# Gate columns, first load buffers and the sums of w_down in a hybrid decoder block

## The chip, the cores and the metric

The kernel runs on one core of one Trainium2 chip. The metric is the device time of one execution in microseconds (us), the median of several runs. The engines of the core are TensorE (PE; its weight loads are listed as PEld), VectorE (DVE), ScalarE (ACT), GpSimd (POOL) and SyncE (SP, which here only issues transfers). Sixteen DMA engines move the data for the queues of SP and POOL.

## What is computed

One layer of a hybrid decoder on x of 512 rows and 1024 columns, float32. Cut to what matters:

```
h = rms_norm(x, norm_mix_g);  p = h @ w_in                  # 1024 x 8208
q_a, k_a, v_a, o_a, i_a, f_a, q_b, k_b, v_b, g_a, g_b = split(p)
y_a = sigmoid(o_a) * head_norm(mlstm(silu(conv(q_a, k_a)), v_a, i_a + b_i, f_a + b_f))
y_b = stick_breaking(head_norm(q_b), head_norm(k_b), v_b)
x = x + (sigmoid(g_a + b) * y_a + sigmoid(g_b + b) * y_b) @ w_out
x = x + square(relu(rms_norm(x, norm_mlp_g) @ w_up)) @ w_down   # 1024 -> 4096 -> 1024
```

## The kernel before

Every float32 matmul operand is cut into a high and a low part in the matmul format (`hi` by a cast on ACT, `lo` by a subtraction on DVE), and a product is made of three matmuls (`mm3`, lines 103 to 105): high by high, high by low, low by high. A slice of weights (256 rows by 512 columns, 512 KB) is loaded by SP into a `raw` buffer, of which there are two, and cut into `whi` and `wlo`, of which there are four each (`stage`, lines 88 to 100).

**The start.** Line 193 loads the gate columns of w_in (16 columns of 1024 rows, tile `wg_r`) on POOL's queue, behind some small vectors. Lines 206 to 210 load the four row tiles of x and, between them, the four slices of the value projection va0 on SP's queue; slices 2 and 3 wait for the buffers of 0 and 1. `norm_rows(t)` normalises row tile t, transposes it on TensorE and cuts it into `hT`. va0 is a product of four parts, one for each row tile, each over all four slices; lines 293 to 303 set norms, parts and gates in their order. `gates` multiplies `hT` by the gate weights `wg`, makes running sums and maxima on DVE and ACT, writes eight rows to DRAM (`rows`) and leaves; each head then has its row broadcast to 128 partitions by POOL's queue (`rb<-rows`, line 363) and takes exponentials of it (line 371). The projections qka0 and qka1 follow va0; each holds four PSUM banks (`pp`, four in all) until ACT has copied them out (`xc`, line 324).

**The MLP.** Four blocks g of 1024 hidden columns. `up(i)` makes 512 hidden columns (i = 0 to 7): 96 matmuls in two halves, then rectifies, squares and cuts the result, with sums and differences of its quadrants, into `ue` (holds A11 and A12), `uf` (A22), `ta` (S1, S4) and `tb` (S2, S3). `down(g)` multiplies by w_down in the Winograd form of Strassen's scheme: seven products instead of eight, each of 24 matmuls, with the numbers and operands of `PRODUCTS` (line 34). The four quadrants B11, B12, B21, B22 of w_down are loaded, each as two slices of 512 KB, into eight buffers `raw_B`; where a product needs a difference of two of them, DVE subtracts in place (line 713), 32 subtractions in all. `parts` (lines 685 to 690) cuts a slice into `whi_p` and `wlo_p`. The sums collect in PSUM in the pairs of banks x, z and y and are added by DVE to the result `acc` or to `s1` (line 730). `ORDER_DOWN` sets the order of the products; 0 stands for the next block's `up(2g+2)`, which is put into the middle of the block, and 9, in the last block, for the additions of s1 to three quadrants.

Within these rules a planner sets the order of the instructions on each engine ahead of time, by priorities (order in the program, less an offset) and by its own simulated times; each engine then runs its list in order.

Of the kernel before, what the change touches and what calls it, by code (L numbers as in the profile page):

```python
# [8 lines left out]
F32 = mybir.dt.float32  # L9
F32R = mybir.dt.float32r  # L10
AF = mybir.ActivationFunctionType
ALU = mybir.AluOpType
# [4 lines left out]
P = 128  # L17
S = 512
D = 1024
NT = S // P  # L20
NK = D // P
# [7 lines left out]
AHEAD = 1500  # L29
# [1 line left out]
NWARM = 5  # L31


PRODUCTS = {1: ("A11", "B11", None, "x", None), 2: ("A12", "B21", None, "x", (0, 0)),
# [3 lines left out]

ORDER_DOWN = (5, 1, 0, 2, 6, 3, 7, 4)
ORDER_LAST = (5, 1, 2, 6, 9, 3, 7, 4)  # L40
C_QA, C_KA, C_VA, C_OA, C_I, C_F = 0, 512, 1024, 2048, 3072, 3080
C_QB, C_KB, C_VB, C_GA, C_GB = 3088, 4112, 5136, 6160, 7184

# [6 lines left out]
def block_kernel(ctx: ExitStack, tc: tile.TileContext, x, norm_mix_g, w_in, b_if, b_gate, conv_w, mlstm_norm_g,  # L50
                 sb_q_norm_g, sb_k_norm_g, w_out, norm_mlp_g, w_up, w_down, out):
    nc = tc.nc
    act, dve, pool, pe = nc.scalar, nc.vector, nc.gpsimd, nc.tensor
# [31 lines left out]

    last = {}

    def stage(k2, srcs, name, ahead=None):

        with tc.high_priority(offset=AHEAD if ahead is None else ahead):  # L90
            raw = wp.tile([P, 2, 512], F32, tag="raw", name=f"raw_{name}{k2}", bufs=2)
            for c, ap in srcs:
                n = ap.shape[-1]
                last["load"] = nc.sync.dma_start(out=raw[:, :, c:c + n],
                                                 in_=ap.rearrange("(kk p) n -> p kk n", p=P)).ins
            hi = wp.tile([P, 2, 512], F32R, tag="whi", name=f"whi_{name}{k2}")
            lo = wp.tile([P, 2, 512], F32R, tag="wlo", name=f"wlo_{name}{k2}")
            act.copy(hi, raw)  # L98
            dve.tensor_sub(lo, raw, hi.bitcast(F32))  # L99
        return hi, lo  # L100
# [88 lines left out]
    nc.gpsimd.dma_start(out=bif[0:8, :], in_=b_if[0, 0:8].rearrange("(p o) -> p o", o=1))  # L189
    nc.gpsimd.dma_start(out=bif[32:40, :], in_=b_if[0, 8:16].rearrange("(p o) -> p o", o=1))  # L190
    vec = cst.tile([P, NV], F32, name="vec")
    wr = cv.tile([P, NK, 16], F32, name="wg_r")
    nc.gpsimd.dma_start(out=wr, in_=w_in[0, :, C_I:C_I + 16].rearrange("(k p) n -> p k n", p=P))

    def col(i):
        return vec[:, i:i + 1]
# [9 lines left out]
    for t in range(NT):  # L206
        xt = xp.tile([P, D], F32, name=f"x_{t}")
        nc.sync.dma_start(out=xt, in_=x[0, t * P:(t + 1) * P, :])
        xs.append(xt)
        va0_w.append(stage(t, va0_src(t), "va0", 0))  # L210
    def norm_rows(t):
        jk = xp.tile([P, D], F32, tag="nx", name=f"jk{t}", bufs=3)
        r = sm.tile([P, 1], F32, tag="r1", name=f"r{t}")
# [78 lines left out]

    norm_rows(0)
    norm_rows(1)
    wg = gate_weights()
    va0 = chunk("va0", None, False, staged=va0_w, evac=v_evac(v0, "va0"), gen=True)
    next(va0)
    norm_rows(2)
    next(va0)
    norm_rows(3)  # L300
    next(va0)
    cc, rows, em = gates(wg)
    next(va0)
# [331 lines left out]
    def up(i):  # L635

        ws, got = [stage(k2, rows2(w_up, 0, i * S)(k2), f"up{i}") for k2 in range(4)], []
        for j in range(2):
            acc = {o: ps_proj.tile([P, S], F32, tag="pp", name=f"pp_up{i}{o}") for o in (j, j + 2)}
            for k in range(NK):  # L640
                for o in acc:
                    sl, (wh, wl) = slice(o * P, (o + 1) * P), ws[k // 2]
                    mm3(acc[o], wh[:, k % 2, sl], wl[:, k % 2, sl], hT[0][:, k, :], hT[1][:, k, :], k == 0, k == NK - 1)
            u = mp.tile([P, 2, S], F32, tag="ur", name=f"ur{i}{j}", bufs=2)
            for w in range(2):
                dve.scalar_tensor_tensor(u[:, w, :], acc[j + 2 * w], 0.0, rw, ALU.max, ALU.mult)  # L646
                act.activation(u[:, w, :], u[:, w, :], AF.Square)  # L647
            e = r4.tile([P, 2, S], F32R, tag="r4", name=f"ue{i}{j}")
            for w in range(2):
                act.copy(e[:, 0, w * 256:w * 256 + 256], u[:, w, HA])  # L650
            e3 = e[:, :, :].rearrange("p x (w n) -> p x w n", w=2)
            dve.tensor_sub(e3[:, 1], u[:, :, HA], e3[:, 0].bitcast(F32))
            f = mp.tile([P, 2, 256], F32R, tag="a22", name=f"uf{i}{j}", bufs=6)
            split(f, u[:, 1, HB])
            sa = big.tile([P, S], F32, tag=f"ya{3 + j}", name=f"sa{i}{j}")
            sb = big.tile([P, S], F32, tag=f"ya{5 + j}", name=f"sb{i}{j}")
            dve.tensor_add(sa[:, HA], u[:, 0, HB], u[:, 1, HB])
            dve.tensor_sub(sb[:, HA], sa[:, HA], u[:, 0, HA])
            dve.tensor_sub(sb[:, HB], u[:, 0, HA], u[:, 0, HB])
            dve.tensor_sub(sa[:, HB], u[:, 1, HA], sb[:, HA])  # L660
            ta = r4.tile([P, 2, S], F32R, tag="r4", name=f"ta{i}{j}")
            split(ta, sa)
            tb = r4.tile([P, 2, S], F32R, tag="r4", name=f"tb{i}{j}")
            made = split(tb, sb)
            got.append({"made": made, "A11": e[:, :, HA], "A12": e[:, :, HB], "A22": f[:, :, :], "S1": ta[:, :, HA],
                        "S4": ta[:, :, HB], "S2": tb[:, :, HA], "S3": tb[:, :, HB]})
        return got

    def quad(r, c, t):
        return acc_t[2 * r + t][:, c * S:(c + 1) * S]  # L670

    def down(g, u):
        raw = {}
        with ExitStack() as es:
            es.enter_context(tc.high_priority(offset=AHEAD))
            if g == 0:
                es.enter_context(tc.issue_after(wo_load))
            for n, r, c in (("B11", 0, 0), ("B12", 0, 1), ("B21", 1, 0), ("B22", 1, 1)):
                for j in range(2):
                    r0 = g * D + (4 * j + 2 * r) * P  # L680
                    raw[n, j] = mp.tile([P, 2, S], F32, tag="rawd", name=f"raw_{n}{g}{j}", bufs=8)
                    nc.sync.dma_start(out=raw[n, j], in_=w_down[0, r0:r0 + 256, c * S:(c + 1) * S]
                                      .rearrange("(kk p) n -> p kk n", p=P))

        def parts(n, t):
            hi = wp.tile([P, 2, S], F32R, tag="whi", name=f"whi_{n}")
            lo = wp.tile([P, 2, S], F32R, tag="wlo", name=f"wlo_{n}")
            act.copy(hi, t)  # L688
            dve.tensor_sub(lo, t, hi.bitcast(F32))  # L689
            return hi, lo  # L690

        order = ORDER_LAST if g == 3 else ORDER_DOWN
        adds = [PRODUCTS[n][4] for n in order if n in PRODUCTS]
        sums = {}
        for n in order:
            if n == 0:
                yield
                continue
            if n == 9:
                for r, c in ((0, 1), (1, 1), (1, 0)):  # L700
                    for t in range(2):
                        dve.tensor_add(quad(r, c, t), quad(r, c, t), s1[t])
                continue
            a, b, diff, to, q = PRODUCTS[n]
            adds.pop(0)
            if diff:
                with ExitStack() as es:
                    if g == 0:
                        es.enter_context(tc.issue_after(last["wo"]))
                    if (g, n) == (3, 4):  # L710
                        es.enter_context(tc.issue_after(u[-1]["made"]))
                    for j in range(2):
                        dve.tensor_sub(raw[b, j], raw[diff[0], j], raw[diff[1], j])  # L713
            with tc.high_priority(offset=AHEAD):
                w = [parts(f"p{n}{g}{j}", raw[b, j]) for j in range(2)]
            start = to not in sums
            if start:
                sums[to] = [bank(f"{to}{g}{t}") for t in range(2)]
            for t in range(2):
                sl = slice(t * P, (t + 1) * P)  # L720
                for p in range(4):
                    (hi, lo), A, kk = w[p // 2], u[p][a], p % 2
                    mm3(sums[to][t], A[:, 0, sl], A[:, 1, sl], hi[:, kk, :], lo[:, kk, :], start and p == 0, p == 3,
                        skip_group_check=True)
            for t in range(2):
                o = s1[t] if q is None else quad(*q, t)
                if n == 1 and g == 0:
                    act.copy(o, sums[to][t])
                else:
                    dve.tensor_add(o, o, sums[to][t])  # L730
                if g == 3 and q and q not in adds:
                    r0, c0 = (2 * q[0] + t) * P, q[1] * S
                    nc.sync.dma_start(out=out[0, r0:r0 + P, c0:c0 + S], in_=o)

    u = up(0) + up(1)
    for g in range(4):
# [31 lines left out]
```

## Time and profile before

| | us |
|---|---|
| median of 3 runs | 848.1 (847.83 to 849.15) |
| the profiled execution | 849.74 |
| its span, first to last instruction | 848.0 |
| TensorE busy | 827.2 |
| DVE busy | 598.6 |
| ACT busy | 408.3 |
| mean granted TensorE clock | 0.992 |

The profile is one execution as the hardware recorded it. Its times are from the start of the span. "Busy" adds up the durations of an engine's instructions. A row of the timeline has start, length, engine, line, operation, what is written from what is read, and in brackets how long the engine stood idle before it and what ended that. TensorE's matmuls overlap, so a matmul of 0.39 us does not mean that the next one starts 0.39 us later.

### The profile page before, as it was taken

The page shows a single profiled execution, that of the slowest core. Times are in us where ns is not written, and L with a number is a line of the kernel's source. Part 1 is how long each engine was busy: PE and PEld are TensorE (multiplying, and loading weights), DVE is VectorE, ACT ScalarE, POOL GpSimd, SP SyncE. Part 2 cuts the span into 40 slices and gives each one's busy share as a digit, 9 for nine tenths or more (in the row PEclk, how much of TensorE's full clock was granted, in tenths as well). Part 3 has the DMA queues.
Part 4 walks back from the last instruction along what each step waited for, and adds up shares of the span by engine and source line. Part 5 has one row for each costly group of instructions (what it writes and reads, how often), then busy time and mean ns, then how long its engine had stood idle before and what let it go on. Part 6 is the DMA issues. An engine that isn't in the chain of part 4 may idle for free.

```text
span 848.0 us, 10083 instructions
## 1 busy us (share of the span) xinstructions
PE 827.2 (98%) x3798; PEld 682.1 (80%) x3798; DVE 598.6 (71%) x808; ACT 408.3 (48%) x619; POOL 84.2 (10%) x150
## 2 busy tenths in 40 slices
PE   5997999999999999999999999999999999999998
PEld 3875888688888788888888888888888888888876
DVE  3484999688647688457465646786958795888695
ACT  4434756846435645355354345553524453453441
POOL 3003045222302011001001100000000000000000
PEclk9998999999999999999999999999999999999999
DMA  7235233333122233222131384211531252226001
GB/s 172 81 102 174 94 116 100 133 95 132 55 99 72 78 83 104 88 83 92 51 120 54 102 321 125 75 48 54 173 124 54 78 183 83 74 75 198 2 25 75
DMA packets 48530, 85.76 MB, mean 101 GB/s; under 512 B 3337, under 2 KB 15673, under 8 KB 48482
## 3 DMA queue, kind: packets, MB, share of 16 engines
q1 hardware_dynamic: 46434, 77.64, 28.8%
q0 software_dynamic: 2048, 7.48, 3.3%
q8 instruction: 30, 0.49, 0.2%
q14 instruction: 18, 0.15, 0.1%
HBM read 82.94 MB, written 2.17 MB: 100 GB/s over the span
## 4 chain that ended last, share of the span: by engine, by line
PE 90%; DMA 4%; DVE 2%; ACT 2%; issue 1%; POOL 1%; SPq 0%; POOLq 0%; ACTq 0%; DVEq 0%
PE pp_up L103 7%; PE pp_up L104 7%; PE pp_up L105 7%; PE pp_qkb L103 3%; PE pp_qkb L104 3%; PE pp_qkb L105 3%; PE y L103 3%; PE y L105 3%; PE y L104 3%; DMA raw_va<-in_w_in_dram 2%; DMA rb<-rows 2%; PE pp_ga L103 2%; PE pp_wo L103 2%; PE pp_ga L105 2%; PE pp_vb L103 2%; PE pp_vb L105 2%
## 5 line engine op out<-in xcount | busy, mean ns | idle before, releaser
L103 PE MATMUL pp_up<-hT,whi_up 128*128 128x512 f32 x256 | 99.3, 390 | 0.0
L104 PE MATMUL pp_up<-hT,whi_up 128*128 128x512 f32 x256 | 99.2, 389 | 0.0
L105 PE MATMUL pp_up<-hT,wlo_up 128*128 128x512 f32 x256 | 94.0, 389 | 0.0
L688 ACT CAST whi_p<-raw_B 128x1024 fp32r<-128x1024 f32 x56 | 59.0, 1055 | 58.4 <-PE pp_up L104 37.8
L689 DVE TENSOR_TENSOR wlo_p<-raw_B,whi_p 128x1024 fp32r<-128x1024 f32 x56 | 68.0, 1221 | 18.0 <-ACT whi_p L688 10.0
L98 ACT CAST whi_up<-raw_up 128x1024 fp32r<-128x1024 f32 x32 | 33.7, 1053 | 60.8 <-PE y L105 28.8
L103 PEld LDWEIGHTS pp_up<-hT,whi_up 128*128 128x128 f32 x256 | 48.0, 188 | 10.5 <-ACT whi_up L98 0.6
L105 PEld LDWEIGHTS pp_up<-hT,wlo_up 128*128 128x128 f32 x256 | 48.1, 188 | 10.0
L104 PEld LDWEIGHTS pp_up<-hT,whi_up 128*128 128x128 f32 x256 | 48.1, 188 | 9.8
L99 DVE TENSOR_TENSOR wlo_up<-raw_up,whi_up 128x1024 fp32r<-128x1024 f32 x32 | 39.1, 1222 | 18.9 <-ACT whi_up L98 18.7
L104 PE MATMUL pp_qkb<-wlo_qkb,hT 128*128 128x512 f32 x128 | 50.0, 391 | 0.0
L103 PE MATMUL pp_qkb<-whi_qkb,hT 128*128 128x512 f32 x128 | 49.8, 393 | 0.2 <-DVE va L161 0.2
L105 PE MATMUL pp_qkb<-whi_qkb,hT 128*128 128x512 f32 x128 | 49.5, 391 | 0.0
L478 POOL TENSOR_SCALAR_AFFINE_SELECT b<-b 128x128 f32<-128x128 f32 x32 | 21.2, 679 | 192.7 <-ACT b L475 115.6
L713 DVE TENSOR_TENSOR raw_B<-raw_B,raw_B 128x1024 f32<-128x1024 f32 x32 | 38.8, 1219 | 0.2
L647 ACT ACTIVATE ur<-ur 128x512 f32<-128x512 f32 x32 | 19.5, 629 | 33.3 <-DVE ur L646 32.9
L483 DVE TENSOR_TENSOR_SCAN r<-r,msk 128x512 f32<-128x512 f32 (+3 forms) x32 | 25.5, 835 | 10.1 <-ACT r L474 10.1
L103 PE MATMUL pp_qka<-hT,whi_qka 128*128 128x512 f32 x64 | 26.0, 408 | 6.2 <-ACT xc L324 6.2
L103 PE MATMUL pp_va<-whi_va,hT 128*128 128x512 f32 x64 | 25.8, 411 | 4.7 <-ACT whi_va L98 4.7
L646 DVE SCALAR_TENSOR_TENSOR ur<-pp_up,rw 128x512 f32<-128x512 f32 x32 | 21.1, 687 | 11.4 <-PE pp_up L105 11.4
L105 PEld LDWEIGHTS pp_qkb<-whi_qkb,hT 128*128 128x128 f32 x128 | 24.0, 188 | 5.6
L103 PEld LDWEIGHTS pp_qkb<-whi_qkb,hT 128*128 128x128 f32 x128 | 24.0, 188 | 5.5 <-DVE va L161 0.5
(286 smaller groups left out, 2235.7 us busy)
## 6 DMA issues: line engine op xcount, KB each, us to landing
raw_B<-in_w_down_dram SPq DMA_DIRECT2D x32, 512.0 KB, 4.2
raw_up<-in_w_up_dram SPq DMA_DIRECT2D x32, 512.0 KB, 4.1
raw_qkb<-in_w_in_dram SPq DMA_DIRECT2D x32, 256.0 KB, 3.8
rb<-rows POOLq DMA_DIRECT2D x8, 640.0 KB, 5.1
raw_va<-in_w_in_dram SPq DMA_DIRECT2D x8, 512.0 KB, 6.7
raw_qka<-in_w_in_dram SPq DMA_DIRECT2D x16, 256.0 KB, 4.7
raw_vb<-in_w_in_dram SPq DMA_DIRECT2D x8, 512.0 KB, 4.1
raw_oa<-in_w_in_dram SPq DMA_DIRECT2D x8, 512.0 KB, 4.0
```

What stands on the lines that cost most here:

```text
L98: act.copy(hi, raw)
L99: dve.tensor_sub(lo, raw, hi.bitcast(F32))
L103: pe.matmul(o, ah, bh, start=start, stop=False, **kw)
L104: pe.matmul(o, ah, bl, start=False, stop=False, **kw)
L105: pe.matmul(o, al, bh, start=False, stop=stop, **kw)
L478: pool.affine_select(out=b[:, d], in_=b[:, d], pattern=[[-1, P]], compare_op=ALU.is_gt, fill=0.0, base=0, channel_multiplier=1)
L483: dve.tensor_tensor_scan(kr, kr, msk[:, S - n:][:, ::-1], 1.0, ALU.mult, ALU.max)
L646: dve.scalar_tensor_tensor(u[:, w, :], acc[j + 2 * w], 0.0, rw, ALU.max, ALU.mult)
L647: act.activation(u[:, w, :], u[:, w, :], AF.Square)
L688: act.copy(hi, t)
L689: dve.tensor_sub(lo, t, hi.bitcast(F32))
L713: dve.tensor_sub(raw[b, j], raw[diff[0], j], raw[diff[1], j])
```

## The change

- The load of the gate columns is taken from POOL's queue at the start and put on SP's queue, in the program behind the loads of x and of va0's slices. The gate weights are made behind norm_rows(3) instead of behind norm_rows(1).
- Slices 0 and 1 of va0 get two `raw` buffers of their own, so that all four slices have one.
- Of w_down only B11, B21 and B22 are loaded, into six buffers X, Z and Y. The operands of products 5, 6, 7 and 4 are made by adding another quadrant to a buffer with a DMA on POOL's queue that adds to what is there (X: B11, then + B12, + B22, + B21; Y: B22, then + B12). Two quadrant sums of the other operand change their sign, and so do three additions to the result.
- The order in a block is 1, 2, 5, 3, 6, the next block's `up`, 7, 4; in the last block 1, 2, 5, 3, the s1 additions, 6, 7, 4.

```diff
-ORDER_DOWN = (5, 1, 0, 2, 6, 3, 7, 4)
-ORDER_LAST = (5, 1, 2, 6, 9, 3, 7, 4)
+PRODUCTS = {1: ("A11", "X", "B11", "x", None, 1), 2: ("A12", "Z", "B21", "x", (0, 0), 1),
+            5: ("S1", "X", "B12", "z", (1, 1), 1), 3: ("S4", "Y", "B22", "z", (0, 1), 1),
+            6: ("S2", "X", "B22", "y", (0, 1), -1), 7: ("S3", "Y", "B12", "y", (1, 1), -1),
+            4: ("A22", "X", "B21", "y", (1, 0), 1)}
+SIGN_1 = {(0, 1): -1, (1, 1): -1, (1, 0): 1}
+ORDER_DOWN = (1, 2, 5, 3, 6, 0, 7, 4)
+ORDER_LAST = (1, 2, 5, 3, 9, 6, 7, 4)
...
-    def stage(k2, srcs, name, ahead=None):
+    def stage(k2, srcs, name, ahead=None, pool_raw=None):
-            raw = wp.tile([P, 2, 512], F32, tag="raw", name=f"raw_{name}{k2}", bufs=2)
+            raw = (pool_raw or wp).tile([P, 2, 512], F32, tag="raw", name=f"raw_{name}{k2}",
+                                        bufs=2)
...
-    wr = cv.tile([P, NK, 16], F32, name="wg_r")
-    nc.gpsimd.dma_start(out=wr, in_=w_in[0, :, C_I:C_I + 16].rearrange("(k p) n -> p k n", p=P))
...
-        va0_w.append(stage(t, va0_src(t), "va0", 0))
+        va0_w.append(stage(t, va0_src(t), "va0", 0, xp if t < 2 else None))
...
     norm_rows(1)
-    wg = gate_weights()
+    wr = cv.tile([P, NK, 16], F32, name="wg_r")
+    nc.sync.dma_start(out=wr, in_=w_in[0, :, C_I:C_I + 16].rearrange("(k p) n -> p k n", p=P))
...
     norm_rows(3)
+    wg = gate_weights()
...
-            for n, r, c in (("B11", 0, 0), ("B12", 0, 1), ("B21", 1, 0), ("B22", 1, 1)):
+            for b, n in (("X", "B11"), ("Z", "B21"), ("Y", "B22")):
                 for j in range(2):
...
-            if diff:
...
-                    for j in range(2):
-                        dve.tensor_sub(raw[b, j], raw[diff[0], j], raw[diff[1], j])
-            with tc.high_priority(offset=AHEAD):
-                w = [parts(f"p{n}{g}{j}", raw[b, j]) for j in range(2)]
+            with tc.high_priority(offset=AHEAD):
+                if n > 3:
+                    for j in range(2):
+                        pool.dma_start(out=buf[b, j], in_=src(more, j), accum_op=ALU.add)
+                w = [parts(f"p{n}{g}{j}", buf[b, j]) for j in range(2)]
```

## Rows read from the trace of the kernel before

**Rows 1.** The page, busy us of each engine (share of the span) x instructions.
```profile
PE 827.2 (98%) x3798; PEld 682.1 (80%) x3798; DVE 598.6 (71%) x808; ACT 408.3 (48%) x619; POOL 84.2 (10%) x150
```
**Rows 2.** Waits of TensorE over the span: us in total, times, longest.
```profile
PE pp_qka L103 <- ACT xc L324: 6.2, 1, 6.2
PE pp_va L103 <- ACT whi_va L98: 4.7, 1, 4.7
PE pt L224 <- DVE xn L220: 2.6, 1, 2.6
...
PE x L103 <- DVE s L730: 0.9, 1, 0.9
```
**Rows 3.** Stretches: length, busy PE, PEld, DVE, ACT, POOL; granted clock, DMA share, GB/s.
```profile
10.00:11.00 1.00, 0.00 (x0) 0.00 (x0) 1.00 (x2) 0.97 (x3) 0.00 (x0) 1.00 1.04 392
...
13.00:14.00 1.00, 1.00 (x5) 0.84 (x4) 1.00 (x3) 0.37 (x2) 0.00 (x0) 1.00 0.00 0
...
20.00:24.00 4.00, 3.56 (x12) 3.04 (x13) 3.33 (x6) 4.00 (x9) 0.00 (x0) 0.50 0.50 172
24.00:48.00 24.00, 24.00 (x110) 19.80 (x109) 12.74 (x20) 8.87 (x13) 0.00 (x0) 0.99 0.17 57
...
78.00:83.00 5.00, 4.91 (x12) 3.91 (x13) 4.93 (x8) 4.25 (x9) 0.17 (x1) 0.53 0.12 43
```
**Rows 4.** DMA queues, first row 0:12, second 11:18: packets, MB, share; landing us.
```profile
q1 hardware_dynamic: 947, 2.61, 58.3%
...
q0 software_dynamic: 20, 0.07, 101.4%
...
wg_r<-in_w_in_dram POOLq DMA_DIRECT2D x1, 64.0 KB, 12.9
```
**Rows 5.** Timeline of the start: start us, us, engine line operation.
```profile
19.34 1.04 ACT L98 CAST whi_va<-raw_va 128x1024 fp32r<-128x1024 f32 x1 [5.97 <-DMA raw_va<-in_w_in_dram]
...
26.06 1.05 ACT L98 CAST whi_va<-raw_va 128x1024 fp32r<-128x1024 f32 x1 [1.57 <-DMA raw_va<-in_w_in_dram]
...
39.37 3.79 PE L247 MATMUL pg<-hT,wg 128*128 128x512 f32 x16
...
48.44 0.39 PE L103 MATMUL pp_qka<-hT,whi_qka 128*128 128x512 f32 x1
```
**Rows 6.** Timeline around the wait at qka1, POOL and ACT.
```profile
62.62 1.61 POOL L363 DMA_DIRECT2D rb<-rows  x3
...
72.90 1.04 ACT L98 CAST whi_qka<-raw_qka 128x1024 fp32r<-128x1024 f32 x1 [7.50 <-DMA raw_qka<-in_w_in_dram]
73.85 3.72 ACT L371 ACTIVATE rb<-rb,cc 128x512 f32<-128x512 f32 x8
```
**Rows 7.** The page: a group of instructions (busy us, mean ns), and DMA landings.
```profile
L713 DVE TENSOR_TENSOR raw_B<-raw_B,raw_B 128x1024 f32<-128x1024 f32 x32 | 38.8, 1219 | 0.2
...
acc<-in_x_dram POOLq DMA_DIRECT2D x4, 512.0 KB, 5.5
```
**Rows 8.** Timeline at the start of the last block, TensorE and DVE.
```profile
804.42 0.39 PE L105 MATMUL pp_up<-hT,wlo_up 128*128 128x512 f32 x1
804.65 0.39 PE L103 MATMUL z<-whi_p,ta 128*128 128x512 f32 x1
...
809.13 0.68 DVE L652 TENSOR_TENSOR ue<-ur,ue 128x512 fp32r<-128x512 f32 x1
...
814.44 1.28 DVE L730 TENSOR_TENSOR s<-s,x 128x512 f32<-128x512 f32 x2
815.27 0.47 PE L103 MATMUL x<-whi_p,ue 128*128 128x512 f32 x1 [0.94 <-DVE s L730]
```
**Rows 9.** Tile raw_B from 520 us on: duration ns min/median/max, and landings.
```profile
L688 ACT CAST whi_p<-raw_B x56: 1037/1056/1062, 551.4 to 833.4; 128x1024 fp32r<-128x1024 f32 x56
L689 DVE TENSOR_TENSOR wlo_p<-raw_B,whi_p x56: 1214/1220/1227, 552.5 to 835.5; 128x1024 fp32r<-128x1024 f32 x56
...
DMA to landing us min/median/max: 3.8/3.9/5.0
```

More of the change, by code (lines that the diff above doesn't have):

```diff
@@ L31 @@
 NWARM = 5
-PRODUCTS = {1: ("A11", "B11", None, "x", None), 2: ("A12", "B21", None, "x", (0, 0)),
[3 rows of a table removed]
-ORDER_DOWN = (5, 1, 0, 2, 6, 3, 7, 4)
-ORDER_LAST = (5, 1, 2, 6, 9, 3, 7, 4)
+PRODUCTS = {1: ("A11", "X", "B11", "x", None, 1), 2: ("A12", "Z", "B21", "x", (0, 0), 1),
[3 rows of a table added]
+SIGN_1 = {(0, 1): -1, (1, 1): -1, (1, 0): 1}
+ORDER_DOWN = (1, 2, 5, 3, 6, 0, 7, 4)
+ORDER_LAST = (1, 2, 5, 3, 9, 6, 7, 4)
 C_QA, C_KA, C_VA, C_OA, C_I, C_F = 0, 512, 1024, 2048, 3072, 3080
@@ L656, in up @@
             sb = big.tile([P, S], F32, tag=f"ya{5 + j}", name=f"sb{i}{j}")
-            dve.tensor_add(sa[:, HA], u[:, 0, HB], u[:, 1, HB])
+            dve.tensor_sub(sa[:, HA], u[:, 0, HB], u[:, 1, HB])
             dve.tensor_sub(sb[:, HA], sa[:, HA], u[:, 0, HA])
             dve.tensor_sub(sb[:, HB], u[:, 0, HA], u[:, 0, HB])
-            dve.tensor_sub(sa[:, HB], u[:, 1, HA], sb[:, HA])
+            dve.tensor_add(sa[:, HB], u[:, 1, HA], sb[:, HA])
             ta = r4.tile([P, 2, S], F32R, tag="r4", name=f"ta{i}{j}")
@@ L672, in down, with src @@
     def down(g, u):
-        raw = {}
+        def src(n, j):
+            r, c = int(n[1]) - 1, int(n[2]) - 1
+            r0 = g * D + (4 * j + 2 * r) * P
+            return w_down[0, r0:r0 + 256, c * S:(c + 1) * S].rearrange("(kk p) n -> p kk n", p=P)
+        buf = {}
         with ExitStack() as es:
@@ L677, in down @@
                 es.enter_context(tc.issue_after(wo_load))
-            for n, r, c in (("B11", 0, 0), ("B12", 0, 1), ("B21", 1, 0), ("B22", 1, 1)):
+            for b, n in (("X", "B11"), ("Z", "B21"), ("Y", "B22")):
                 for j in range(2):
[L680 to L683, printed above, removed]
+                    buf[b, j] = mp.tile([P, 2, S], F32, tag="rawd", name=f"raw_{b}{g}{j}", bufs=8)
+                    nc.sync.dma_start(out=buf[b, j], in_=src(n, j))
         def parts(n, t):
@@ L690, in parts, with add @@
             return hi, lo
+        def add(o, val, sign):
+            (dve.tensor_add if sign > 0 else dve.tensor_sub)(o, o, val)
         order = ORDER_LAST if g == 3 else ORDER_DOWN
@@ L699, in down @@
             if n == 9:
-                for r, c in ((0, 1), (1, 1), (1, 0)):
+                for q, sign in SIGN_1.items():
                     for t in range(2):
-                        dve.tensor_add(quad(r, c, t), quad(r, c, t), s1[t])
+                        add(quad(*q, t), s1[t], sign)
                 continue
-            a, b, diff, to, q = PRODUCTS[n]
+            a, b, more, to, q, sign = PRODUCTS[n]
             adds.pop(0)
-            if diff:
[L707 to L711, printed above, removed]
+            with tc.high_priority(offset=AHEAD):
+                if n > 3:
                     for j in range(2):
-                        dve.tensor_sub(raw[b, j], raw[diff[0], j], raw[diff[1], j])
-            with tc.high_priority(offset=AHEAD):
-                w = [parts(f"p{n}{g}{j}", raw[b, j]) for j in range(2)]
+                        pool.dma_start(out=buf[b, j], in_=src(more, j), accum_op=ALU.add)
+                w = [parts(f"p{n}{g}{j}", buf[b, j]) for j in range(2)]
             start = to not in sums
@@ L725, in down @@
             for t in range(2):
-                o = s1[t] if q is None else quad(*q, t)
-                if n == 1 and g == 0:
-                    act.copy(o, sums[to][t])
+                if q is None and g == 0:
+                    act.copy(s1[t], sums[to][t])
                 else:
-                    dve.tensor_add(o, o, sums[to][t])
+                    add(s1[t] if q is None else quad(*q, t), sums[to][t], sign)
                 if g == 3 and q and q not in adds:
                     r0, c0 = (2 * q[0] + t) * P, q[1] * S
-                    nc.sync.dma_start(out=out[0, r0:r0 + P, c0:c0 + S], in_=o)
+                    nc.sync.dma_start(out=out[0, r0:r0 + P, c0:c0 + S], in_=quad(*q, t))
     u = up(0) + up(1)
```

3 rows, old and new, of the table PRODUCTS are left out of this document.

## The prediction, made before the changed kernel was run

> **What bounds the kernel now.** I read the busy times first [rows 1]: TensorE is busy 827.2 of 848.0 us, no other engine more than 71%. So the kernel can only get shorter where TensorE stands still or runs at its lower clock, and longer where a new wait reaches it. Then the waits of TensorE [rows 2]: 6.2 us at one place in the projection qka1, 4.7 us at one place in the first product va0, 2.6 us before a transpose, and in the whole MLP (from about 522 us to the end) a single wait of 0.9 us. The MLP is where most of the diff's lines are, and it has almost nothing to give. The start has.
>
> Next, what lies behind the two large waits. From 10 to 11 us the loads move 392 GB/s; from 13 to 17 us nothing moves at all [rows 3] (the row of 13 to 14 us is the first of four alike). The queue table of 11 to 18 us says why: 0.07 MB on the POOL queue took 101% of all 16 DMA engines' time, about 7 us [rows 4]. The only transfer of that queue with this size is the gate columns (line 193): 1024 rows of 16 floats, 64 bytes each. While its packets stand on the engines, raw_va of slice 1, issued on SP's queue ahead of it, can't land, and its cast starts at 19.34 us after 5.97 us of idle ACT [rows 5]. TensorE idles till then, and the granted clock falls to 0.50, the lower of its two levels (1.2 against 2.4 GHz), and is still there from 20 to 24 us [rows 3]: 12 instructions in 3.56 us, half of which the upper level would have saved. Slices 2 and 3 come later still, since they wait for the two raw buffers (last cast 26.06). From the end of that cast, 20.4 us, TensorE runs va0, transposes and gates without a wait (24.00 of 24.00 us busy from 24 to 48 us [rows 3]) until qka0 begins at 48.4; the gate product pg starts at 39.4 [rows 5].
>
> The second wait is another matter [rows 6]: qka1 needs the four banks of qka0, their copies (line 324) stand on ACT [rows 2] behind a cast that waits 7.50 us for raw_qka, and behind eight exponentials that wait for three row broadcasts issued at 62.62 us. TensorE starts again at 78 us, at 0.53 of its clock until 83 [rows 3].
>
> **The change, part by part.**
>
> *Gate columns and first buffers.* The load moves from POOL's queue to SP's, behind x and the four raw_va loads, which now wait for no buffer. What is queued behind it on SP are raw_qka loads, issued from 24.62 us on and cast only from 44 us on; even 7 us of the same slow packets, ending at about 23 us, are covered by that. Its own reader, the gate product, runs after the third product of va0, 15 us later; moving the four small DVE operations and the memset of the gate weights behind norm_rows(3) is covered by the same distance. Without the dead time the loads end as follows: 2.6 MB had moved by 12 us [rows 4], of 4.2 MB for x and the four slices; the other 1.6 MB at 400 GB/s take 4 us. So all is there at 15 to 16 us, where the last cast now starts at 26.06. Then DVE is the feeder: between 14 and 23 us it owes three subtractions of 1.22 us, the norm multiplications and the transposed halves, and the last wlo of va0 comes at 22 to 23 us instead of after the cast at 26.06, at 28.6. TensorE's work from 20.4 to 48.4 is 28.0 us, of which the half clock is 1.8 to 2.0, so 26 us at full rate. It can begin at 14.5 to 15 us and loses 1 to 3 us in waits for slices 2 and 3; it ends at 42 to 44 us. Gain: 4.4 to 6.4 us; I take **5.5**. As outer ends 2 us (TensorE gets the early slices but a feeder stops it for another 3 us, and the clock falls again) and 7 us (4.7 idle and 2.0 clock, and some of the 2.6).
>
> *What the gain meets.* The gate product, the row broadcasts and qka0 all move forward by the same amount: the chain from the gate product to the exponentials and the chain of qka0 on TensorE start at the same place. So the 6.2 us and the 2 us at half clock behind it stay: **0**, with ends of 8 us gained and 3 us lost, because the broadcasts' landing sets them.
>
> *The sums of w_down.* Removed are 32 DVE subtractions of 1.22 us, 38.8 us in all, and 8 loads of SP [rows 7]. TensorE waits for DVE once in the whole MLP, so I cost the removal at nothing. Added are 32 DMAs of 512 KB on POOL's queue, 4 pairs for each block; POOL has 10% busy time and nothing of it in the MLP, so issuing is free. Each pair waits until ACT and DVE have read the old content of its buffer; queued behind it on POOL are only the next adding DMAs, and waiting for it are the casts (line 688) on ACT and the subtractions on DVE, with all that stands behind them in those queues. How late may a pair be? Matmuls start 0.23 us apart [rows 8], so a product of 24 takes 5.5 us. Four whi buffers hold two products, so the parts of a product can be made when the product two places ahead has read its first pair of slices (18 of 24 matmuls, 4.1 us); cast and subtraction take 1.05 and 1.22 us [rows 9], so they are done 4.6 us before their product starts. From there to the next use of X, two products on, less the 2.3 us of its own parts, is 4.6 + 11.0 - 2.3 = **13 us**. A plain load of this size lands in 3.9 us (5.0 at most) on SP [rows 9] and in 5.5 us (median) as one of four from POOL [rows 7]. No row shows an adding DMA. Lower end 3.9, upper end two passes of the slower row, 11 us: both lie inside 13. I take 5.5 to 8 us and cost **0**. Traffic rises from 32 to 56 transfers of 512 KB here; the 12.6 MB more are some 32 us at the rate of [rows 3], spread over 320 us.
>
> The Trainium skill (Collectives: The Full Stack, section "The bandwidth ceiling: the fold count and why AG ≠ RS ≠ AR") says that an add in the DMA engine costs no time as such, but that two sources are read through one ring, which halves the rate (62.28 against 32.35 GB/s). By that a pair would land in about 1.93 x 5.5 = 10.6 us (an estimate from that page and [rows 7]); the sum would be the same, with little room left. No run here shows it yet.
>
> *The new order.* Products 1 and 2 now stand side by side in every block, and both accumulate in the banks x with the addition to s1 between them. Before, only the last block had that, and there lies the 0.9 us: the s1 additions started at 814.44 and TensorE at 815.27 [rows 8]. In the other blocks the next up projection filled the time. Now its first half stands after product 6, so nothing fills it. With a free DVE: s1 starts 0.3 us after the first half of product 1, TensorE may go on 0.8 us after that, and covering it are the last three matmuls of the second half, 0.7 us: 0.4 to 0.5 us of wait in each of four blocks. With one subtraction of 1.22 us ahead of it: 1.1 us or more. Product 1 needs the last ue piece as well: up ended at 804.65, ue at 809.8 [rows 8], 5.2 us, of which 1.2 was a removed subtraction; the 18 matmuls on the other pieces cover 4.1. So 4 x 0.5 - 0.9 = about **+1.0 us**; ends -0.9 (no wait anywhere) and +8 (2.2 us in each block). The banks of y are free earlier than before, and there was no wait there.
>
> **Sum.** 5.5 - 0 - 0 - 1.0 = 4.5 us less. The profiled execution took 849.7 (span 848.0 and 1.7 around it), the median of the three runs is 848.1; the parts are in us of the span, and I take them off the median: **843.6 us**, with 841 to 846.4 as the forecast's own range.
>
> **Rivals.**
> 1. *The adding DMAs are late* (slower). The mechanism is the X buffer: products 1, 5 and 6 follow each other with one product between, and in the last block product 4 too, so nine sums are on a short path. It decides from 13 us of landing on, with every us above costing up to 9 us. At twice the longest landing in [rows 9] and the issue of a pair, 11 us, it costs nothing; at 14 us, 9 us: 853; at 15, 862. For it: nothing in the trace shows the rate of an add, and ACT and DVE would stand still behind the wait. Against: the 13 us are over twice the slowest row. With it I count products 1 and 2 costing over 2.1 us in each block, which gives 850 and more. Chance 0.20.
> 2. *The start gains little.* The gate load's slow packets come ahead of slices 2 and 3, or the feeders on ACT and DVE are the next bound with an idle TensorE and its lower clock again. Gain 0 to 2, less 1: 847 to 849. For it: DVE is already full at 10 and 13 us [rows 3]. Against: the loads stand before it in SP's queue. Chance 0.14.
> 3. *The second wait goes too.* If the broadcasts meet fewer raw_qka loads, up to 6.2 + 2 us: 836 to 840. For it: the planner places the casts, exponentials and copies anew. Against: both chains move together. Chance 0.13.
>
> The forecast has 0.53. A measurement of this kernel tells about 0.2% (1.7 us) from no change. Faster by more: the forecast, rival 3 and a little of rival 2, 0.66; within: 0.14; slower: 0.20. The range of 838 to 853 leaves out half of rival 3 and the worse part of rival 1.
>
> **What would show it.** Right: no dead time on the DMA engines at 13 to 17 us, all four casts of raw_va before 21 us, qka0 beginning at 42 to 44 us, the wait at qka1 still some 6 us, TensorE's waits on x of half a us in four places of the MLP, adding DMAs landing within 11 us. Wrong: TensorE or ACT waiting for adding DMAs of raw_B, a low granted clock inside the MLP, or the first qka matmul at 47 us or later.

## The result and the profile after

| | before | after |
|---|---|---|
| median (lowest to highest) | 848.56 (847.83 to 849.15) | 840.01 (838.94 to 840.96) |
| the profiled execution, its span | 849.74, 848.0 | 838.94, 837.2 |

The ratio is 0.9899, with a 95% interval of 0.9882 to 0.9917: 8.5 us less. The forecast was 843.6, with a range of 838 to 853. The time lies in that range, but below the 841 to 846.4 that the forecast gave as its own, and it was not made up as the forecast said. All that follows is in us.

The page of the changed kernel first, then TensorE's waits over the whole span (us in total, times, longest).

```profile
PE 823.9 (98%) x3798; PEld 679.3 (81%) x3798; DVE 564.0 (67%) x776; ACT 408.9 (49%) x619; POOL 125.9 (15%) x181
...
L719 POOL DMA_DIRECT2D raw_X<-in_w_down_dram x24 | 29.0, 1209 | 287.6 <-DVE wlo_p L696 285.7
...
raw_X<-in_w_down_dram POOLq DMA_DIRECT2D x24, 512.0 KB, 6.3
```

```profile
PE pt L226 <- DVE xn L222: 2.3, 1, 2.3
PE pp_va L107 <- DVE nat L445: 1.7, 1, 1.7
PE y L107 <- DVE acc L700: 1.5, 1, 1.5
...
PE pn L107 <- ACT ph L393: 1.5, 2, 0.8
PE z L108 <- DVE wlo_p L696: 0.5, 3, 0.2
```

Both large waits of [rows 2] are gone, the one in va0 and the one at qka1. In their place stand small ones: those on `nat` (between 112 and 115 us) and on `acc` and `wlo_p` (in the MLP) were not there before, and that on `ph` (up to 146 us) was a single one of 0.5. DVE lost the 32 subtractions of [rows 7] (38.8 us; over all its work it is busy 34.6 us less), and POOL issues the adding DMAs at 1.21 us each.

Stretches of the changed kernel (length; busy PE, PEld, DVE, ACT, POOL; granted clock, DMA share, GB/s) are to be compared with [rows 3].

```profile
10.00:11.00 1.00, 0.00 (x0) 0.00 (x0) 1.00 (x3) 0.97 (x4) 0.00 (x0) 1.00 0.98 377
13.00:14.00 1.00, 1.00 (x7) 1.00 (x6) 1.00 (x2) 0.97 (x3) 0.00 (x0) 1.00 0.89 303
17.00:24.00 7.00, 7.00 (x37) 5.87 (x36) 5.44 (x8) 2.67 (x6) 0.00 (x0) 1.00 0.07 10
78.00:83.00 5.00, 5.00 (x23) 4.13 (x22) 4.92 (x7) 2.46 (x4) 0.00 (x0) 1.00 0.22 63
557.00:563.00 6.00, 6.00 (x29) 4.95 (x28) 3.38 (x5) 2.11 (x2) 1.80 (x2) 1.00 1.10 197
```

At 13 to 14 us the loads still move 303 GB/s where nothing moved before. The gate columns now go from 17 to 24 us at 10 GB/s beside a fully busy TensorE. At 20 to 24 and 78 to 83 us the granted clock is 1.00 where it was 0.50 and 0.53. The last row belongs to the adding DMAs, below.

The timeline of the start is to be compared with [rows 5].

```profile
17.66 1.06 ACT L102 CAST whi_va<-raw_va 128x1024 fp32r<-128x1024 f32 x1 [0.31 <-DMA raw_va<-in_w_in_dram]
...
33.17 0.39 PE L249 MATMUL pg<-hT,wg 128*128 128x512 f32 x1
...
41.11 0.39 PE L107 MATMUL pp_qka<-hT,whi_qka 128*128 128x512 f32 x1
...
87.45 0.40 PE L107 MATMUL pp_qkb<-whi_qkb,hT 128*128 128x512 f32 x1
...
501.67 0.47 PE L107 MATMUL pp_up<-hT,whi_up 128*128 128x512 f32 x1
```

The last cast of va0 starts 8.4 us earlier than in [rows 5] (17.66 against 26.06) and qka0 7.3 us earlier (41.11 against 48.44); the gate product `pg` gained only 6.2 us (33.17 against 39.37). The last two rows are the first matmul behind qka1 and the first of the MLP. The kernel before has them here:

```profile
103.41 0.40 PE L103 MATMUL pp_qkb<-whi_qkb,hT 128*128 128x512 f32 x1
...
514.58 0.47 PE L103 MATMUL pp_up<-hT,whi_up 128*128 128x512 f32 x1
```

So TensorE is ahead by 7.3 at qka0, by 16.0 behind qka1, by 12.9 at the MLP and by 10.8 at the end of the span. That is the ledger: start -7.3, the wait at qka1 and its half clock **-8.6**, given back between qka1 and the MLP +3.0, MLP +2.1. It compares one execution of each kernel. In the seven other traces with the new start qka0 begins at 41.0 to 42.1 us and the MLP at 501.5 to 502.9, in `mlp_only`, which has the old start, at 50.9 and 517.0; so an entry before the MLP is good to 1 or 2 us.

### The profile page after: what moved, and what is told of

Same layout as the page of the kernel before. It is cut to its first block, busy times and chain, and to the rows that moved or that the text cites. A ratio compares the mean times of both kernels' runs of the same rounds, so it can differ in the third digit from the quotient of the medians.

```text
span 837.2 us, 10133 instructions
## 1 busy us (share of the span) xinstructions
PE 823.9 (98%) x3798; PEld 679.3 (81%) x3798; DVE 564.0 (67%) x776; ACT 408.9 (49%) x619; POOL 125.9 (15%) x181
## 4 chain that ended last, share of the span: by engine, by line
PE 47%; issue 37%; DMA 6%; DVE 5%; POOL 4%; ACT 1%; POOLq 0%; SPq 0%; DVEq 0%; ACTq 0%
DMA raw_X<-in_w_down_dram 5%; PE pp_qkb L107 3%; PE pp_qkb L109 3%; PE pp_qkb L108 3%; POOL raw_X L719 2%; PE pp_ga L107 2%; PE pp_vb L107 2%; PE pp_ga L109 2%; PE pp_ga L108 2%; PE pp_vb L108 2%; PE pp_gb L107 2%; PE pp_oa L107 2%; PE pp_gb L108 2%; PE pp_vb L109 2%; PE pp_oa L108 2%
## 5 line engine op out<-in xcount | busy, mean ns | idle before, releaser
L109 PE MATMUL pp_up<-hT,wlo_up 128*128 128x512 f32 x256 | 96.2, 389 | 0.0
L719 POOL DMA_DIRECT2D raw_X<-in_w_down_dram x24 | 29.0, 1209 | 287.6 <-DVE wlo_p L696 285.7
L695 ACT CAST whi_p<-raw_X 128x1024 fp32r<-128x1024 f32 x32 | 33.8, 1056 | 37.7 <-PE pp_up L108 24.9
L696 DVE TENSOR_TENSOR wlo_p<-raw_X,whi_p 128x1024 fp32r<-128x1024 f32 x32 | 39.1, 1223 | 6.1 <-ACT whi_p L695 5.9
L108 PEld LDWEIGHTS pp_qkb<-wlo_qkb,hT 128*128 128x128 f32 x128 | 24.0, 188 | 5.3
L695 ACT CAST whi_p<-raw_Y 128x1024 fp32r<-128x1024 f32 x16 | 16.9, 1053 | 21.5 <-PE x L109 13.8
```

Of the source, the lines that this page charges most:

```text
L108: pe.matmul(o, ah, bl, start=False, stop=False, **kw)
L109: pe.matmul(o, al, bh, start=False, stop=stop, **kw)
L719: pool.dma_start(out=buf[b, j], in_=src(more, j), accum_op=ALU.add)
```

## Experiments

**Taking the change apart.** `gate_only` moves the gate load and the making of `wg` alone, `bufs_only` adds the two buffers alone, `start_both` does both and leaves the MLP as before, and `mlp_only` is the changed kernel with the start put back.

```diff
-    nc.gpsimd.dma_start(out=wr, in_=w_in[0, :, C_I:C_I + 16].rearrange("(k p) n -> p k n", p=P))
...
     norm_rows(1)
-    wg = gate_weights()
+    nc.sync.dma_start(out=wr, in_=w_in[0, :, C_I:C_I + 16].rearrange("(k p) n -> p k n", p=P))
...
     norm_rows(3)
+    wg = gate_weights()
```

is the edit of `gate_only`, and that of `bufs_only` is

```diff
-        va0_w.append(stage(t, va0_src(t), "va0", 0))
+        va0_w.append(stage(t, va0_src(t), "va0", 0, xp if t < 2 else None))
```

`start_both` has both, and `mlp_only` takes both back from the changed kernel.

> The kernel before with the gate columns on SP's queue behind x and the slices, the gate weights made behind norm_rows(3); two raw buffers and the MLP as before. Theory (the 7 us of dead time come from the packets of this load alone): no dead time, slices 2 and 3 still wait for buffers but land by about 20 us, qka0 begins at 42 to 44 us instead of 48.4; the planner's list for ACT has the copies of qka0 between the exponentials, so the wait at qka1 falls from 6.2 to under 4 us: 838 to 843 us. Rival (the buffers are what delays the slices, the dead time only shifts the blame): qka0 not before 46 us, 845 to 848 us.

Measured: 844.11, ratio 0.9942 (0.9923 to 0.9962).

> The kernel before with two more raw buffers for slices 0 and 1 of va0, all else as before. Theory (the gate columns' packets stand in front of everything from 11 to 18 us): the dead time stays, slices 1 to 3 land at 19 to 23 us, the last cast comes at 22 to 23 instead of 26 us, but TensorE had work from 20.4 us on without a wait, so qka0 begins at 47 to 48.4 us and the wait at qka1 stays near 6 us: 846.5 to 848.5 us. Rival (the buffers are the main term): qka0 at 44 us or earlier, under 844 us.

Measured: 848.37, ratio 1.0001 (0.9989 to 1.0012).

> Both changes of the start, the MLP of the kernel before. Theory (all of the gain and more is made before the MLP; the MLP part costs 2 us): TensorE's rows up to the MLP as in the changed kernel (qka0 at 41.1 us, no wait at qka1), MLP of before: 836.5 to 839 us. Rival (the MLP part is neutral or a gain): 840 us or more.

Measured: 837.27, ratio 0.9862 (0.9844 to 0.9880).

> The start of the kernel before, the MLP of the changed kernel (six buffers, adding DMAs, new order). Theory: the start keeps its waits of 4.7 and 6.2 us, the MLP takes some 2 us longer than before (a wait of 1.5 us in the last block, three of 0.3 us in the others, against one of 0.9 us before): 849.5 to 852 us. Rival (neutral or a gain): 848.5 us or less.

Measured: 852.0, ratio 1.0029 (1.0014 to 1.0044).

Alone, the load saves 4.6 us and the buffers nothing; together they save 11.4. `gate_only` came out between its two theories: qka0 begins at 45.10 us there (49.01 in `bufs_only`, 41.50 in `start_both`). The timelines of ACT say why, `gate_only` first:

```profile
22.14 1.04 ACT L98 CAST whi_va<-raw_va 128x1024 fp32r<-128x1024 f32 x1 [5.53 <-DMA raw_va<-in_w_in_dram]
24.40 1.05 ACT L98 CAST whi_va<-raw_va 128x1024 fp32r<-128x1024 f32 x1 [0.24 <-DMA raw_va<-in_w_in_dram]
```

Without the buffers SP issues the gate columns at 5.09 us and slices 2 and 3 only from 10.70 us on, so that they wait out the small rows on their own queue; slice 2 is late by 5.53 us of idle ACT. In `bufs_only` the loads are issued early but the gate columns are still on POOL's queue, and slice 1 lands late as before:

```profile
19.59 1.04 ACT L99 CAST whi_va<-raw_va 128x1024 fp32r<-128x1024 f32 x1 [6.11 <-DMA raw_va<-in_w_in_dram]
```

The buffers put the slices ahead of the gate columns, and only then is the new place of the gate columns free of cost.

Of TensorE's waits at `xc` (6.2 in [rows 2]) `gate_only` keeps one of 4.2 us, `bufs_only` one of 4.8, `mlp_only` one of 6.3; `start_both` has none. In `start_both` qka0 begins 6.9 us earlier than before, and qkb, at 88.01, 15.4 earlier.

**Why the wait at qka1 went.** In the kernel before, slice 2 of qka1 is issued at the moment of the row broadcasts (timeline, SP and POOL):

```profile
62.62 1.09 POOL L363 DMA_DIRECT2D rb<-rows  x2
62.68 0.88 SPq L94 DMA_DIRECT2D raw_qka<-in_w_in_dram  x2
```

In the changed kernel the slice goes out 2.6 us ahead of them, and no wait of ACT in these rows is longer than 2.04 us (timeline, SP, POOL and ACT):

```profile
54.85 0.88 SPq L98 DMA_DIRECT2D raw_qka<-in_w_in_dram  x2
...
57.46 1.63 POOL L367 DMA_DIRECT2D rb<-rows  x3
...
59.10 1.05 ACT L102 CAST whi_qka<-raw_qka 128x1024 fp32r<-128x1024 f32 x1 [1.03 <-DMA raw_qka<-in_w_in_dram]
62.19 1.53 ACT L375 ACTIVATE rb<-rb,cc 128x512 f32<-128x512 f32 x3 [2.04 <-POOL rb L369]
63.62 0.56 ACT L328 COPY xc<-pp_qka 128x512 f32<-128x512 f32 x1
```

The slice moved by 7.8 us, the broadcasts by 5.2. From the slice's issue to its cast it takes 4.3 us, where it took 10.2 (62.68 to 72.90), and the cast that waited 7.50 us in [rows 6] waits 1.03. But a second thing changed: the copies of `xc` no longer stand behind eight exponentials on ACT but behind three. Two experiments on the kernel before take one of the two each. `slice_own` loads slice 2 into two idle tiles, issued behind the last load of qka0:

```diff
+        if (name, k2) == ("qka1", 2):
+            own = (ya[6], ya[7])
+            with tc.issue_after(last["qka0", 3]), tc.high_priority(offset=AHEAD):
...
+                    nc.sync.dma_start(out=own[w][:, c:c + ap.shape[-1]], in_=ap[w * P:(w + 1) * P, :])
...
+                    act.copy(hi[:, w, :], own[w])
+                    dve.tensor_sub(lo[:, w, :], own[w], hi[:, w, :].bitcast(F32))
```

> The kernel before, except that slice 2 of qka1 has buffers of its own (two tiles not yet in use) and is loaded right behind qka0's last slice, so it doesn't meet the three row broadcasts; ACT's list is unchanged, the eight exponentials still stand in front of qka0's copies. Theory (the wait at qka1 is this slice's collision with the broadcasts, which holds ACT for 7.5 us): its cast starts at some 66 us instead of 72.9, ACT is free for the exponentials as the broadcasts land, TensorE's wait falls from 6.2 to 2 to 4 us, with less time at the lower clock: 843 to 846 us. Rival (ACT's order alone makes the wait): wait still 5 to 6 us, 847.5 to 849 us.

Measured: 846.89, ratio 0.9972 (0.9960 to 0.9984). `copies_first` leaves the loads and puts the exponentials of three heads behind the copies:

```diff
+            elif h < 3:
+                es.enter_context(tc.issue_after(last["xc", 0]))
```

> The kernel before, except that the exponentials of the first three broadcasts stand behind qka0's copies in ACT's list; the loads are unchanged. Theory (collision): the copies still stand behind the cast that waits for slice 2 until 72.9 us; they start at 74 instead of 77.5 us, so the wait at qka1 falls from 6.2 to about 2.7 us: 843.5 to 845.5 us. Rival (order alone): no wait at qka1, 840 us or less.

Measured: 845.28, ratio 0.9954 (0.9940 to 0.9967). SP and ACT in `slice_own`:

```profile
62.21 0.88 SPq L107 DMA_DIRECT2D raw_qka<-in_w_in_dram  x2
...
66.34 1.14 ACT L100 CAST whi_qka<-ya 128x512 fp32r<-128x512 f32 x2 [1.48 <-PE pp_qka L118]
...
71.93 1.92 ACT L385 ACTIVATE rb<-rb,cc 128x512 f32<-128x512 f32 x4 [1.53 <-POOL rb L379]
73.76 1.53 ACT L338 COPY xc<-pp_qka 128x512 f32<-128x512 f32 x3
```

and in `copies_first`:

```profile
73.10 1.04 ACT L98 CAST whi_qka<-raw_qka 128x1024 fp32r<-128x1024 f32 x1 [7.62 <-DMA raw_qka<-in_w_in_dram]
74.06 1.56 ACT L324 COPY xc<-pp_qka 128x512 f32<-128x512 f32 x3
```

Each cause alone holds the copies until about 74 us instead of 77.48: in the one the cast is on time and the exponentials wait for their broadcasts, in the other the exponentials are out of the way and the cast waits 7.62 us. TensorE's wait falls to 2.4 and 2.1. So both causes are real and each covers a part of the other. `slice_own` took less off the time than its theory said, and it doesn't free the broadcasts: with slice 2 out of the way slice 3 goes out at 62.21 us (first row above), just ahead of the broadcasts at 62.39, and POOL reads the last of them 11.0 us after that, much as in the kernel before (11.2); in the changed kernel it is 8.5. No run joins the two edits, so that together they make up the whole 6.2 us is read from the changed kernel's trace, not shown by a run.

The order on ACT comes with the gate load: `bufs_only` still has eight exponentials in front of the copies, `gate_only` four. Its slice is cast in time, yet it keeps 4.2 us of the wait, since the broadcasts, issued at 61.91, come late (timeline of ACT):

```profile
64.36 1.05 ACT L98 CAST whi_qka<-raw_qka 128x1024 fp32r<-128x1024 f32 x1 [5.33 <-DMA raw_qka<-in_w_in_dram]
70.33 1.92 ACT L371 ACTIVATE rb<-rb,cc 128x512 f32<-128x512 f32 x4 [4.92 <-POOL rb L365]
72.16 0.56 ACT L324 COPY xc<-pp_qka 128x512 f32<-128x512 f32 x1
```

Why the planner puts the copies earlier then was not tried.

**What the MLP part costs.** The changed kernel and `start_both` again, timed side by side.

> The changed kernel again, on the same chip as the three kernels that follow, so that small differences to it can be told. Every theory: 839 to 841 us, 0.990 of the kernel before.

Measured: 840.12, ratio 0.9904 (0.9883 to 0.9925).

> The start of the change (gate load and first buffers) with the MLP of the kernel before. Theory that the MLP part costs: 836.5 to 838.5 us, 2 to 3 us below the changed kernel, since TensorE's starts in the MLP of the changed kernel's trace lose 2.1 us. Rival, that the MLP part costs nothing and the first difference was chance of the chip: within 1 us of the changed kernel.

Measured: 836.99, ratio 0.9863 (0.9845 to 0.9882). The MLP part costs 3.1 us here and 2.5 by its ratio (3.3 by the medians) on top of the old start (`mlp_only`). `start_both` is faster than both kernels. Its whole MLP has one wait of 0.9 us (on `s`, as in [rows 2]), while `mlp_only` shows in its MLP three of 0.5 us in total on `wlo_p`, as in the changed kernel, and

```profile
PE y L107 <- DVE acc L700: 1.6, 1, 1.6
```

From its first to its last matmul the MLP takes 329.3 us in the traces of the kernel before, `start_both` and `start_both_5`, and 331.5 to 331.9 in those of the changed kernel, `after_5` and `mlp_only`. The wait above stands in the last block, in front of product 7; `s1_early` tests it.

```diff
-ORDER_LAST = (1, 2, 5, 3, 9, 6, 7, 4)
+ORDER_LAST = (1, 9, 2, 5, 3, 6, 7, 4)
```

> The changed kernel with the additions of s1 in the last block put right behind product 1 instead of behind product 3. The changed kernel's TensorE waits 1.5 us once, for an addition to the result in front of product 7. Theory that the six additions of s1 stand before that one on DVE: 838 to 839 us. Rival, that the additions only move and then delay DVE's subtractions of the weight slices of products 2, 5 or 3: 840 to 844 us.

Measured: 839.19, ratio 0.9888 (0.9870 to 0.9906). The wait on `acc` (2.0 in `after_5`'s trace) is gone, and one of 0.6 on `wlo_p` has come, in front of product 6; the rival named such a wait, but for other products. By the medians 0.9 us are gained against `after_5`; the two intervals overlap, so the trace tells this better than the time.

**What the adding DMAs are worth.** `dve_adds` keeps the new order and makes the same sums on DVE, with B12 loaded as well.

```diff
-                        pool.dma_start(out=buf[b, j], in_=src(more, j), accum_op=ALU.add)
+                        o = {5: "W", 6: "Y", 7: "W", 4: "Z"}[n]
+                        dve.tensor_add(buf[b, j], buf[b, j], buf[o, j])
```

> The changed kernel with its order and signs, but all four quadrants of w_down are loaded by SP into eight buffers, and DVE makes the 32 sums in place instead of the adding DMAs. Theory (what the MLP lost is the order: products 1 and 2 side by side, the s1 additions in front of product 7 in the last block; the adding DMAs are hidden): no gain from taking them away, and DVE has 38.8 us more to do, 840 to 844 us. Rival (the adding DMAs cost the 2 us): 837 to 838.5 us.

Measured: 847.22, ratio 0.9975 (0.9966 to 0.9985), slower than either theory had it. TensorE's waits in its last three blocks (600 us to the end):

```profile
PE y L107 <- DVE acc L700: 2.7, 3, 1.2
PE x L107 <- DVE s L700: 1.7, 3, 0.6
PE z L108 <- DVE wlo_p L696: 1.1, 3, 0.4
PE y L108 <- DVE wlo_p L696: 0.6, 1, 0.6
```

In the old order TensorE is busy 80.00 of 80 us between 600 and 680 with all the subtractions on DVE (`start_both`); in the new order with the additions on DVE 78.99. In the new order the adding DMAs are worth some 6 us (0.9904 against 0.9975). In the old one they were not run; its MLP waits for DVE 0.9 us in all, so there is little for them to win.

**How late may a sum be?** `add_twice` issues each adding DMA twice, so that the added quadrant counts double, and `adds_late` holds each pair back by a copy on POOL and moves no byte more by DMA.

```diff
 add_twice
                         pool.dma_start(out=buf[b, j], in_=src(more, j), accum_op=ALU.add)
+                        pool.dma_start(out=buf[b, j], in_=src(more, j), accum_op=ALU.add)
 adds_late
+                    pool.tensor_copy(buf[b, 0], buf[b, 0])
                     for j in range(2):
                         pool.dma_start(out=buf[b, j], in_=src(more, j), accum_op=ALU.add)
```

> The changed kernel with every adding DMA issued twice, the second behind the first (the operands of products 5, 6, 7 and 4 then hold a quadrant twice, so the output is not the reference's). Measures the room behind an adding DMA: it lands 6.3 us after its issue (median), the pair of them some 13 to 14. Theory (13 us of room): 840 to 848 us, waits of a us or two at products 5 and 6. Rival (room of 8 us or less): each of nine sums 5 us late or more, over 875 us.

Measured: 895.99, ratio 1.0556 (1.0535 to 1.0576).

> The changed kernel with a GpSimd copy of the first slice onto itself ahead of each pair of adding DMAs, so that both are issued later by the copy (1.5 to 4 us, no row shows one of this size) and no byte more is moved. My prediction gave a pair 13 us from issue to use; a pair lands in about 9 us in the changed kernel's trace, so 1.5 to 4 us more would cost nothing or next to nothing: 839.5 to 842 us. Against it, the trace of the changed kernel shows only 3.4 and 2.6 us (product 5) and 2.0 and 1.6 us (product 6) between landing and cast of the slices: by that, with a copy of 3 us, about 1 us at nine places, 845 to 852 us.

Measured: 872.92, ratio 1.0281 (1.0258 to 1.0304).

The timeline of a pair for product 5 in the changed kernel (POOL issues, ACT casts):

```profile
622.43 1.20 POOL L719 DMA_DIRECT2D raw_X<-in_w_down_dram  x1 [54.77 <-DVE wlo_p L696]
625.63 1.21 POOL L719 DMA_DIRECT2D raw_X<-in_w_down_dram  x1 [2.00 <-DVE wlo_p L696]
...
632.09 1.06 ACT L695 CAST whi_p<-raw_X 128x1024 fp32r<-128x1024 f32 x1
634.13 1.05 ACT L695 CAST whi_p<-raw_X 128x1024 fp32r<-128x1024 f32 x1 [0.98 <-PE x L109]
...
634.97 1.20 POOL L719 DMA_DIRECT2D raw_X<-in_w_down_dram  x1 [8.13 <-DVE wlo_p L696]
...
645.49 1.06 ACT L695 CAST whi_p<-raw_X 128x1024 fp32r<-128x1024 f32 x1 [1.21 <-PE z L109]
```

With the median landing of 6.3 us the second slice is there at 631.9, and the casts begin when TensorE has freed their `whi` buffers, not on a DMA. From the first issue to the second cast there are 11.7 us (634.13 less 622.43), for product 6 10.5 (the last two rows); the pair takes about 9.5. The same place in `add_twice` (POOL, ACT, TensorE):

```profile
541.17 1.27 POOL L719 DMA_DIRECT2D raw_X<-in_w_down_dram  x1 [70.09 <-DVE wlo_p L696]
...
557.06 1.04 ACT L695 CAST whi_p<-raw_X 128x1024 fp32r<-128x1024 f32 x1 [7.34 <-DMA raw_X<-in_w_down_dram]
559.67 1.05 ACT L695 CAST whi_p<-raw_X 128x1024 fp32r<-128x1024 f32 x1
...
558.15 1.22 PE L107 MATMUL z<-whi_p,ta 128*128 128x512 f32 x2 [5.82 <-ACT whi_p L695]
```

and in `adds_late` (POOL, ACT, TensorE):

```profile
631.76 1.17 POOL L718 COPY raw_X<-raw_X 128x1024 f32<-128x1024 f32 x1 [53.01 <-DVE wlo_p L696]
635.91 2.44 POOL L720 DMA_DIRECT2D raw_X<-in_w_down_dram  x2 [2.98 <-DVE wlo_p L696]
...
646.75 1.99 ACT L695 CAST whi_p<-raw_X 128x1024 fp32r<-128x1024 f32 x2 [5.16 <-DMA raw_X<-in_w_down_dram]
...
647.85 0.73 PE L107 MATMUL z<-whi_p,ta 128*128 128x512 f32 x2 [4.20 <-ACT whi_p L695]
```

The copy took 1.17 us, but behind it both transfers waited for the subtraction of the second slice as well, so the first was late by 3 us more than the copy. The second cast starts 16 us after the copy, and TensorE has waited 4.20 us for the first; in `add_twice` the second cast starts 18.5 us after the first issue, and TensorE has waited 5.82. Less these waits both leave 12 to 13 us of room (an estimate from these rows).

Against the changed kernel the two runs lose 33 and 56 us. TensorE's waits for the casts of product 5 over the whole MLP, `adds_late` first and `add_twice` behind it, are

```profile
PE z L107 <- ACT whi_p L695: 16.2, 4, 4.9
PE z L107 <- ACT whi_p L695: 16.0, 4, 5.8
```

and all its waits in the MLP 23 and 41 us, of which 8.3 in `add_twice` are a single one on `acc`. The rest is about what the lower clock costs: the mean granted clock of the two spans is 0.988 and 0.981, against 1.00 in the changed kernel, which is 10 and 17 us. From the one run to the other the loss grows by 23 us for 2.5 us of delay, about nine for each. The time of `add_twice` is the one that its rival gave (over 875 us), but the room of 8 us or less that it was to come from is not what the rows show.

## Why the prediction was right or wrong

**The start: right, 1.8 us too small.** 7.3 against 5.5, just over the outer end of 7 for the beginning of qka0 at 41.11 (said: 42 to 44). All loads and casts came as the text said (last cast 17.66, "before 21"), and TensorE lost less than the 1 to 3 us set aside for waits on slices 2 and 3: from 13 to 40 us it is busy without a gap (27.00 of 27.00). That the two edits need each other was said only in part: the text covers the gate load's new place on SP's queue by the raw_qka loads behind it, and that cover exists only with the buffers.

**The wait at qka1: wrong, and the largest error.** The step that failed is "all move forward by the same amount", with **0** for the wait. The gate product moved 6.2 us, the broadcasts 5.2, TensorE's qka0 7.3 and the slice for qka1 7.8, so the slice came to lie 2.6 us ahead of the broadcasts and went through the DMA engines first. Rival 3 named this case ("if the broadcasts meet fewer raw_qka loads", and an order of ACT placed anew) at a chance of 0.13. It happened; I should have seen that in the kernel before slice and broadcasts are issued within a tenth of a us (62.68 and 62.62), so that no shift of several us could be taken to leave them where they were. I also read the chain as one queue of causes, while `slice_own` and `copies_first` show two that each cover a part of the other.

**What was not in the sum: 3.0 us given back.** Between 112 and 146 us TensorE now waits for DVE's `nat` and ACT's `ph` (1.7 and 1.5 in the waits above, against none and 0.5 before). TensorE came 16 us earlier to work that is fed through ACT and DVE, which did not gain as much. I had no line for a wait that a large gain uncovers behind it. Which feeder is late there was read from the trace, not tested.

**The sums by adding DMAs: cost 0 was right, its margin was not.** The room of 13 us was nearly right (the casts came 10.5 and 11.7 us after the first issue in the rows, and the two runs give 12 to 13). The landing of a pair was not: 9.5 against "5.5 to 8". So the margin was 1 to 3 us instead of 5 or more, and rival 1 was closer than its chance of 0.20 tells; its slope of nine us for each us came out, though the lower clock, which it did not count, has a share in it. One of the signs of being wrong did come: ACT waited for adding DMAs twice, 3.1 us in all, for product 4 of the last block (casts at 819.57 and 822.14), but TensorE began that product only at 827.97 and did not wait. The estimate from the Trainium skill (Collectives: The Full Stack, "The bandwidth ceiling: the fold count and why AG ≠ RS ≠ AR") was 10.6 for a pair, nearer to what came, in part by chance, since 3.2 of the 9.5 us lie between the two issues. The trace agrees with the halved rate: 197 GB/s with the engines full of adding DMAs, 377 with plain loads (stretches above). My later expectation of little loss in `add_twice` and in `adds_late` failed as well: I doubled and shifted the landings without following what POOL's queue waits for in between.

**The removed subtractions: "worth nothing" holds for the old order alone.** In the new one the sums on DVE cost some 6 us (`dve_adds`), and TensorE waits for DVE at `acc`, `s` and `wlo_p`.

**The new order: +2.1 instead of +1.0, by another mechanism.** The four waits on x did not come, because the planner put matmuls of product 5 between products 1 and 2 (14 of them from 633.93 us on). Instead a wait of 1.5 us came in the last block on `acc`, with the s1 additions ahead of it on DVE, and three small ones on `wlo_p`. These idle times, 2.0 less the 0.9 of before, are only half of the +2.1, because the matmuls right behind a wait start further apart than 0.23 us too: by the starts in the traces the wait on `acc` costs 1.8 us and each of the three some 0.5, against 1.2 for the one on `s` before. `after_5` against `start_both_5` puts the whole MLP part at 3.1.

So -4.5 was forecast and -10.8 came in the span, as -7.3, -8.6, +3.0 and +2.1. The medians differ by 8.5, since the profiled execution of before was 1.2 us above its median and that of after 1.1 below. The time is at the upper end of rival 3's 836 to 840, and that it still lies in the stated range is luck: a gain that I had at 0 was eaten to more than half by two losses, of which I had only one in the sum, at half its size.

## What to carry to other kernels

Where two transfers are issued within a tenth of a us of each other and one of them ends a wait, a shift of the chains in front decides which is first; cost such a wait at both values, not at 0. An edit that moves a slow transfer to another queue is only free once what stood behind it there has gone ahead, so the edits are to be costed together. And an operation taken off an engine with room is worth nothing until something else is changed that fills that engine: here the new order with its sums on DVE is some 9 us slower than the old one (0.9975 against 0.9863), the adding DMAs take some 6 of them back, and the start alone is the faster kernel (836.99 against 840.12).

## What the hardware showed

- The same 64 KB of gate columns, in rows of 64 bytes, held all 16 DMA engines for about 7 us on POOL's queue (101.4% in [rows 4]) and still moved for about 7 us on SP's, but with a share of 0.07 of the engines (17 to 24 us above). What stood behind them on SP's own queue waited there too (`gate_only`).
- An adding DMA moves half of what a plain load does (197 against 377 GB/s with full engines), lands 512 KB in 6.3 us against 3.9 in [rows 9], and takes POOL 1.21 us to issue, against 0.54 for a broadcast (1.61 for three in [rows 6]).
